# The first two k-tiles' weights on ScalarE's DMA queue, in a one-core encoder block

## Chip, cores and metric

The kernel runs on one core of one Trainium2 chip. The metric is device time in microseconds (us): the median of 3 runs of the whole program, 980.93 us for the kernel before (980.78 to 981.23).

## The reference

One layer of a streaming encoder on 512 positions with 1024 channels (`x` is 1 x 512 x 1024, float32). Cut to its start, which is where the change lies:

```
hn   = rms_norm(h, g_mix_pre)             # h = x, per position over 1024 channels
proj = hn @ w_in                          # 1024 x 8192, split among the mixers
a, gate = split(z_conv); h_conv = a * sigmoid(gate)     # columns 2048..4095 of w_in
...   # spatial gating, causal conv of width 31, multi-scale pooling, three gates,
      # output projection, SwiGLU (2816 wide), per-layer input embedding
```

The normalisation's factor is one number per position, so a product with `x * g_mix_pre` can start before it is known and be scaled afterwards. The kernel does that for the first 6 column blocks of the conv projection.

## The kernel before, in words

**Layout.** Channels lie on the 128 partitions, positions (512) on the free axis. A contraction over 1024 channels is 8 k-tiles of 128. TensorE multiplies float32 values as two rounded parts, high and low: each product is three matmuls (high by high, weight-high by x-low, weight-low by x-high), so each weight and each activation tile is split once: ScalarE rounds the high part (`CAST` or `ACTIVATE`), VectorE subtracts to get the low one.

**The start.** TensorE first runs 9 warm-up matmuls on zeros (`ps_warm`, 8 of 512 columns and one of 256). Meanwhile the inputs arrive: `vec` (the gains, L132, issued by ScalarE), 8 k-tiles of x (`x_all`, 256 KB each, L140) and 8 k-tiles of the first weights (`first_all` and `first_raw`, 384 KB each, L143), issued by SyncE in one hand-written order: the table `X_AHEAD = (1, 2, 4, 8, ...)` says how many tiles of x go ahead of each weight tile. The weights of k-tile 0 come in two cuts (128 KB and 256 KB), so that the first two column blocks can start on the smaller. Below, w0a and w0b are these two cuts, w1 the weights of k-tile 1, x0 to x7 the tiles of x; all land in their own place, and a DMA signals one of 8 semaphores (DMAHW0 to DMAHW7) taken in turn in program order, so that the ninth DMA waits until the first has landed.

**The first product.** `first_product(k, passes)` adds k-tile k to six PSUM banks (`ps_first`): six matmuls weight-high by x-high, six weight-high by x-low, six weight-low by x-high, 18 in all. For k-tile 0 the two column blocks of w0a go through all three passes first (6 matmuls), then the four of w0b (12). `x_high(k)` on ScalarE writes the high part of x times gain (`xg`), `x_low(k)` on VectorE the low one, `w_split(k)` splits the weights, `x_square(k)` adds the square of x to the statistics (`sq`, `x_sums`). All of them run in program order on each engine:

```
x_high(1); w_split(1); x_low(1); x_square(1); x_square(2)
first_product(1, passes)
```

So VectorE's order for k-tile 1 is: low part of w1, then low part of xg1; and ScalarE's is xg1 high, then w1 high. After k-tile 3 the statistics go through `ps_stat`, and the program goes on with the other weights, which SyncE loads one block at a time (L199).

Of the kernel before, what the change touches and what calls it, by code (L numbers as in the profile page):

```python
# [85 lines left out]
def hybrid_block(  # L86
# [7 lines left out]
    nc = tc.nc  # L94
# [19 lines left out]
    def slot(tag, name, dt=F32R, shape=(2, T)):  # L114
        return act.tile([P, *shape], dt, tag=tag, name=name, bufs=6 if tag == "tm" else 8)
# [11 lines left out]
    first_raw = []  # L127

    def first_cuts(k):
        return ((0, 2 * P), (2 * P, N_FIRST)) if k == 0 else ((0, N_FIRST),)  # L130
# [3 lines left out]
    for k in range(KT):  # L134
        if k < 5:
            first_raw.append(first_all[:, k * N_FIRST:(k + 1) * N_FIRST])
        else:
            first_raw.append(slot("hn", "first_raw", F32, (D,))[:, :N_FIRST])
        while x_ahead < X_AHEAD[k]:
            nc.sync.dma_start(out=x_all[:, x_ahead], in_=xT[:, x_ahead])  # L140
            x_ahead += 1
        for c0, c1 in first_cuts(k):
            nc.sync.dma_start(out=first_raw[k][:, c0:c1], in_=w_first[k][:, c0:c1])  # L143

    def col(name, k):
        i = VECS.index(name) * KT + k
# [775 lines left out]
    with order():  # L922
# [19 lines left out]
        c0, c1 = ffn_out_cuts[1]  # L942
# [10 lines left out]
        k = 0  # L953
# [92 lines left out]
```

## Time and profile before

| what | value |
|---|---|
| runs | 980.78, 980.93, 981.23 us; median 980.93 |
| profiled execution, own time | 980.2 us |
| its span | 978.4 us |
| TensorE busy | 971.8 us, 99% of the span |
| VectorE, ScalarE busy | 69%, 36% |
| TensorE granted clock | 1.0 in every slice |
| DMA moved | 102.76 MB, mean 105 GB/s |

The span runs from the first to the last instruction that the profiler saw; the run's own time holds 1.8 us more around it. PE is TensorE's matmul, PEld its weight load, DVE VectorE, ACT ScalarE, SP SyncE. All matmuls and splits go through one helper, so they all show line L73, and groups are told apart by tile names (`xg`, `first`, `ps_first`). Times in a timeline are us from the span's start. The ends of matmuls are modelled; the starts of weight loads are the better clock of TensorE's progress.

### The profile page before, as it was taken

The page shows a single profiled execution, that of the slowest core. Times are in us where ns is not written, and L with a number is a line of the kernel's source. Part 1 is how long each engine was busy: PE and PEld are TensorE (multiplying, and loading weights), DVE is VectorE, ACT ScalarE, POOL GpSimd, SP SyncE. Part 2 cuts the span into 40 slices and gives each one's busy share as a digit, 9 for nine tenths or more (in the row PEclk, how much of TensorE's full clock was granted, in tenths as well). Part 3 has the DMA queues.
Part 4 walks back from the last instruction along what each step waited for, and adds up shares of the span by engine and source line. Part 5 has one row for each costly group of instructions (what it writes and reads, how often), then busy time and mean ns, then how long its engine had stood idle before and what let it go on. Part 6 is the DMA issues. An engine that isn't in the chain of part 4 may idle for free.

```text
span 978.4 us, 11730 instructions
## 1 busy us (share of the span) xinstructions
PE 971.8 (99%) x4683; PEld 818.0 (84%) x4683; DVE 672.4 (69%) x905; ACT 350.4 (36%) x487; POOL 83.8 (9%) x63
## 2 busy tenths in 40 slices
PE   9999999999999999999999999999999999999998
PEld 6888888788888888888888998888888888888897
DVE  7987789999988899967555777544454432223575
ACT  7522323432214432247326433323232322223442
POOL 1100013000013702160000010000000000000000
PEclk9999999999999999999999999999999999999999
DMA  8723322222222222332337112232323233334312
GB/s 305 195 93 102 113 87 72 100 86 96 99 86 90 96 95 92 102 110 85 108 123 264 45 44 86 88 107 86 108 86 108 84 99 97 100 86 138 110 42 86
DMA packets 30726, 102.76 MB, mean 105 GB/s; under 512 B 3536, under 2 KB 4048, under 8 KB 30672
## 3 DMA queue, kind: packets, MB, share of 16 engines
q1 hardware_dynamic: 29808, 99.75, 31.1%
q0 software_dynamic: 720, 2.23, 1.2%
q8 instruction: 36, 0.59, 0.2%
q14 instruction: 18, 0.15, 0.0%
q10 hardware_dynamic: 144, 0.04, 0.0%
HBM read 97.68 MB, written 2.10 MB: 102 GB/s over the span
## 4 chain that ended last, share of the span: by engine, by line
PE 94%; DVE 4%; issue 1%; ACT 0%
PE ps_f L73 25%; PE ps_gate L73 13%; PE ps_br L73 13%; PE ps_fo L73 12%; PE ps_ag L73 6%; PE ps_pg L73 5%; PE ps_o L73 5%; PE ps_z L73 4%; PE ps_nat L73 4%; PE ps_first L73 3%; DVE lo L73 1%; DVE acc L73 1%; PE ps_ple L73 1%; PE ps_pool L73 1%; DVE v_all L73 1%
## 5 line engine op out<-in xcount | busy, mean ns | idle before, releaser
L73 ACT CAST hi<-raw 128x1024 fp32r<-128x1024 f32 (+2 forms) x157 | 161.6, 1031 | 455.9 <-PE ps_br L73 83.6
L73 DVE TENSOR_TENSOR lo<-raw,hi 128x1024 fp32r<-128x1024 f32 (+2 forms) x155 | 203.9, 1317 | 107.8 <-ACT hi L73 107.3
L73 DVE SCALAR_TENSOR_TENSOR acc<-h_conv,vec,acc 128x511 f32<-128x511 f32 (+14 forms) x240 | 183.4, 764 | 5.2
L73 PE MATMUL ps_f<-hg,hi 128*128 128x512 f32 (+1 forms) x624 | 184.3, 378 | 0.0
L73 PEld LDWEIGHTS ps_f<-hg,hi 128*128 128x128 f32 x624 | 115.1, 188 | 21.8
L73 PE MATMUL ps_gate<-hn,hi 128*128 128x512 f32 x384 | 119.6, 392 | 0.9 <-DVE gated L73 0.9
L73 PE MATMUL ps_f<-hg,lo 128*128 128x512 f32 (+1 forms) x312 | 117.8, 378 | 0.0
L73 PE MATMUL ps_fo<-f,hi 128*128 128x512 f32 (+1 forms) x396 | 111.0, 366 | 0.0
L73 PEld LDWEIGHTS ps_gate<-hn,hi 128*128 128x128 f32 x384 | 71.9, 188 | 17.0 <-DVE gated L73 1.3
L73 PEld LDWEIGHTS ps_fo<-f,hi 128*128 128x128 f32 x396 | 71.7, 189 | 12.2
L73 PE MATMUL ps_nat<-hi,hn 128*128 128x512 f32 x256 | 78.9, 389 | 0.0
L73 PE MATMUL ps_gate<-hn,lo 128*128 128x512 f32 x192 | 74.8, 389 | 0.0
L73 PE MATMUL ps_fo<-f,lo 128*128 128x512 f32 (+1 forms) x198 | 72.4, 365 | 0.0
L73 PEld LDWEIGHTS ps_f<-hg,lo 128*128 128x128 f32 x312 | 58.7, 188 | 10.9
L73 PEld LDWEIGHTS ps_nat<-hi,hn 128*128 128x128 f32 x256 | 48.0, 188 | 10.1
L73 DVE TENSOR_TENSOR f<-ps_f,h_inv 128x512 f32<-128x512 f32 x22 | 15.2, 690 | 56.5 <-PE ps_f L73 56.5
L73 PE MATMUL ps_nat<-lo,hn 128*128 128x512 f32 x128 | 49.8, 389 | 0.0
L73 PE MATMUL ps_ag<-hn,hi 128*128 128x512 f32 x160 | 49.2, 389 | 0.0
L73 PEld LDWEIGHTS ps_gate<-hn,lo 128*128 128x128 f32 x192 | 36.0, 188 | 7.5
L73 PEld LDWEIGHTS ps_fo<-f,lo 128*128 128x128 f32 x198 | 37.3, 189 | 5.9
L73 DVE TENSOR_TENSOR silu<-ps_f,h_inv 128x512 f32<-128x512 f32 x22 | 15.2, 690 | 36.3 <-PE ps_f L73 36.2
L73 PE MATMUL ps_br<-pool,hi 128*128 128x512 f32 x128 | 39.6, 389 | 0.0
(221 smaller groups left out, 1561.2 us busy)
## 6 DMA issues: line engine op xcount, KB each, us to landing
raw<-in_w_mix SPq DMA_DIRECT2D x90, 512.0 KB, 3.3
raw<-in_w_ffn_in SPq DMA_DIRECT2D x44, 512.0 KB, 3.3
raw<-in_w_ffn_out SPq DMA_DIRECT2D x16, 448.0 KB, 3.3
raw<-in_w_ffn_out SPq DMA_DIRECT2D x8, 512.0 KB, 3.6
raw<-in_w_ple_gate SPq DMA_DIRECT2D x8, 512.0 KB, 3.8
x_all<-in_xT SPq DMA_DIRECT2D x8, 256.0 KB, 6.4
h_all<-in_xT SPq DMA_DIRECT2D x4, 512.0 KB, 5.5
out_dram<-pg SPq DMA_DIRECT2D x7, 256.0 KB, 2.0
```

The source lines that it names most:

```text
L73: inst = op(*args, **kw)
```

## The change

For k-tiles 0 and 1 the weight DMAs are issued by ScalarE instead of SyncE. That is three DMAs: w0a, w0b and w1.

```diff
         while x_ahead < X_AHEAD[k]:
             nc.sync.dma_start(out=x_all[:, x_ahead], in_=xT[:, x_ahead])
             x_ahead += 1
+        queue = nc.scalar if k < 2 else nc.sync
         for c0, c1 in first_cuts(k):
-            nc.sync.dma_start(out=first_raw[k][:, c0:c1], in_=w_first[k][:, c0:c1])
+            queue.dma_start(out=first_raw[k][:, c0:c1], in_=w_first[k][:, c0:c1])
```

ScalarE at the program's start, before the change (the number in front is the place in the engine's order; `waits` names semaphores; `xg_126` is xg0, `xg_127` xg1):

```order
1 L132 DMA vec<-in_vecs 128x72
2 L73 ACT_TABLE_LOAD
3 L73 COPY warm<-mean_mat 128x1 [waits DVE_49]
4 L73 ACTIVATE xg_126<-x_all,vec 128x512 [waits DMAHW1_49,DMAHW0_49]
5 L73 CAST first<-first_all 128x512 [waits DMAHW3_49]
6 L73 ACTIVATE x_sums<-x_all 128x512
7 L73 ACTIVATE xg_127<-x_all,vec 128x512 [waits DMAHW4_49]
8 L73 CAST first<-first_all 128x768 [waits DMAHW5_49]
```

ScalarE at the same place with the change:

```order
1 L132 DMA vec<-in_vecs 128x72
2 L144 DMA first_all<-in_w_first 128x256
3 L144 DMA first_all<-in_w_first 128x512
4 L144 DMA first_all<-in_w_first 128x768
5 L73 ACT_TABLE_LOAD
6 L73 COPY warm<-mean_mat 128x1 [waits DVE_49]
7 L73 ACTIVATE xg_126<-x_all,vec 128x512 [waits DMAHW1_49,DMAHW0_49]
8 L73 CAST first<-first_all 128x512 [waits DMAHW5_49]
9 L73 ACTIVATE x_sums<-x_all 128x512
10 L73 ACTIVATE xg_127<-x_all,vec 128x512 [waits DMAHW2_49]
11 L73 CAST first<-first_all 128x768 [waits DMAHW7_49]
```

The three issues stand behind `vec` and ahead of the table load, the warm copy and the first `xg`.

SyncE at the program's start, before the change:

```order
1 L140 DMA x_all<-in_xT 128x512
2 L143 DMA first_all<-in_w_first 128x256
3 L143 DMA first_all<-in_w_first 128x512
4 L140 DMA x_all<-in_xT 128x512
5 L143 DMA first_all<-in_w_first 128x768
6 L140 DMA x_all<-in_xT 128x512 x2
7 L143 DMA first_all<-in_w_first 128x768 [waits DMAHW0_49]
8 L140 DMA x_all<-in_xT 128x512 [waits DMAHW1_49]
9 L140 DMA x_all<-in_xT 128x512 [waits DMAHW2_49]
10 L140 DMA x_all<-in_xT 128x512 [waits DMAHW3_49]
11 L140 DMA x_all<-in_xT 128x512 [waits DMAHW4_49]
12 L143 DMA first_all<-in_w_first 128x768 [waits DMAHW5_49]
```

SyncE at the same place with the change:

```order
1 L140 DMA x_all<-in_xT 128x512 x4
2 L144 DMA first_all<-in_w_first 128x768 [waits DMAHW0_49]
3 L140 DMA x_all<-in_xT 128x512 [waits DMAHW1_49]
4 L140 DMA x_all<-in_xT 128x512 [waits DMAHW2_49]
5 L140 DMA x_all<-in_xT 128x512 [waits DMAHW3_49]
6 L140 DMA x_all<-in_xT 128x512 [waits DMAHW4_49]
7 L144 DMA first_all<-in_w_first 128x768 [waits DMAHW5_49]
```

x0 to x3 now stand next to each other; behind them the order of SyncE's DMAs is as before. The semaphores of the first eight DMAs are dealt out in another order (x1 takes DMAHW2, x2 DMAHW4, x3 DMAHW6, w0a DMAHW3, w0b DMAHW5, w1 DMAHW7); the rows from the ninth on wait for the same numbers as before. The orders of TensorE, VectorE and GpSimd are unchanged.

## Rows read from the trace of the kernel before

**Rows 1.** The page: busy time by engine, the granted clock in 40 slices, and the chain that ended last, by engine.

```profile
PE 971.8 (99%) x4683; PEld 818.0 (84%) x4683; DVE 672.4 (69%) x905; ACT 350.4 (36%) x487; POOL 83.8 (9%) x63
...
PEclk9999999999999999999999999999999999999999
...
PE 94%; DVE 4%; issue 1%; ACT 0%
```

**Rows 2.** The chain in order of time, 0 to 45 us: start us, us, what.

```profile
1.34 3.81 PE ps_warm L73 x9
5.14 15.38 PE ps_first L73 x66
20.52 0.86 PE ps_stat L73 x2
```

**Rows 3.** Timeline of PEld: start us, us, operation, and in brackets the idle time before it with what ended it. The first rows are of 1 to 6 us; the others are the 19th and the 25th weight load of the first product, each asked for by its own short stretch.

```profile
1.74 0.15 PEld L73 LDWEIGHTS <-warm_up 128*128 128x128 bf16 x1 [0.28 <-issue]
2.16 0.15 PEld L73 LDWEIGHTS <-warm_up 128*128 128x128 bf16 x1 [0.28 <-issue]
...
4.81 0.50 PEld L73 LDWEIGHTS ps_first<-xg,first 128*128 128x128 f32 x2 [0.36 <-ACT xg L73]
5.71 14.38 PEld L73 LDWEIGHTS ps_first<-xg,first 128*128 128x128 f32 x64 [0.40 <-DVE xg L73]
...
9.25 0.19 PEld L73 LDWEIGHTS ps_first<-xg,first 128*128 128x128 f32 x1
...
10.61 0.19 PEld L73 LDWEIGHTS ps_first<-xg,first 128*128 128x128 f32 x1
```

**Rows 4.** Timeline of ScalarE, 0 to 9 us, same columns (ACTq is its DMA issue).

```profile
0.74 0.41 ACTq L132 DMA_DIRECT2D vec<-in_vecs  x1
1.18 1.28 ACT L73 ACT_TABLE_LOAD   x1 [1.18 <-PEq L1034]
2.47 0.19 ACT L73 COPY warm<-mean_mat 128x1 f32<-128x1 f32 x1
4.04 0.72 ACT L73 ACTIVATE xg<-x_all,vec 128x512 fp32r<-128x512 f32 x1 [1.38 <-DMA vec<-in_vecs]
4.88 0.62 ACT L73 CAST first<-first_all 128x512 fp32r<-128x512 f32 x1
...
7.00 0.72 ACT L73 ACTIVATE xg<-x_all,vec 128x512 fp32r<-128x512 f32 x1 [0.96 <-DMA x_all<-in_xT]
7.98 0.83 ACT L73 CAST first<-first_all 128x768 fp32r<-128x768 f32 x1 [0.26 <-DMA first_all<-in_w_first]
```

**Rows 5.** Timeline of VectorE, 3 to 11 us, same columns.

```profile
4.24 0.29 DVE L73 CAST first<-first_all 128x256 fp32r<-128x256 f32 x1 [2.56 <-DMA first_all<-in_w_first]
4.57 0.43 DVE L73 TENSOR_TENSOR first<-first_all,first 128x256 fp32r<-128x256 f32 x1
4.92 0.75 DVE L73 SCALAR_TENSOR_TENSOR xg<-x_all,vec,xg 128x512 fp32r<-128x512 f32 x1
...
8.85 0.96 DVE L73 TENSOR_TENSOR first<-first_all,first 128x768 fp32r<-128x768 f32 x1 [2.58 <-ACT first L73]
9.72 0.74 DVE L73 SCALAR_TENSOR_TENSOR xg<-x_all,vec,xg 128x512 fp32r<-128x512 f32 x1
```

**Rows 6.** Timeline of SyncE's DMA issues, 0 to 12 us, its first ones: start us, us, what, how many.

```profile
0.74 0.39 SPq L140 DMA_DIRECT2D x_all<-in_xT  x1
1.19 0.90 SPq L143 DMA_DIRECT2D first_all<-in_w_first  x2
2.12 0.43 SPq L140 DMA_DIRECT2D x_all<-in_xT  x1
2.60 0.43 SPq L143 DMA_DIRECT2D first_all<-in_w_first  x1
3.07 0.91 SPq L140 DMA_DIRECT2D x_all<-in_xT  x2
4.03 0.42 SPq L143 DMA_DIRECT2D first_all<-in_w_first  x1
```

**Rows 7.** DMA issues by line in short stretches: queue, how many, KB each, us from issue to landing. In order: x0 (issued at 0.74), w0a (1.19), vec (0.74); w0b (1.66); x1 and w1 (2.12 and 2.60, in one answer); w2 and x3 (4.03 and 3.55, in one answer).

```profile
x_all<-in_xT SPq DMA_DIRECT2D x1, 256.0 KB, 3.1
first_all<-in_w_first SPq DMA_DIRECT2D x1, 128.0 KB, 3.0
vec<-in_vecs ACTq DMA_DIRECT2D x1, 36.0 KB, 3.3
...
first_all<-in_w_first SPq DMA_DIRECT2D x1, 256.0 KB, 3.2
...
first_all<-in_w_first SPq DMA_DIRECT2D x1, 384.0 KB, 5.4
x_all<-in_xT SPq DMA_DIRECT2D x1, 256.0 KB, 4.9
...
first_all<-in_w_first SPq DMA_DIRECT2D x1, 384.0 KB, 6.7
x_all<-in_xT SPq DMA_DIRECT2D x1, 256.0 KB, 6.2
```

**Rows 8.** DMA traffic. First, what was moved in each of 40 slices of 0 to 10 us (0.25 us each, GB/s); then the two queues in the stretch 2.5 to 3.0 us (q1 is SyncE's, q10 ScalarE's): packets, MB, share of the 16 DMA engines.

```profile
GB/s 0 0 0 0 0 0 0 158 100 226 232 330 367 314 371 393 328 197 49 131 197 160 217 270 332 377 356 324 295 295 307 262 287 332 328 352 414 418 406 414
...
q1 hardware_dynamic: 80, 0.12, 71.5%
q10 hardware_dynamic: 63, 0.02, 15.1%
```

**Rows 9.** Timeline of PE, 184 to 190 us: an idle stretch before a matmul and the matmuls after it.

```profile
185.52 0.72 PE L73 MATMUL ps_gate<-hn,hi 128*128 128x512 f32 x2 [0.88 <-DVE gated L73]
186.08 0.40 PE L73 MATMUL ps_gate<-hn,lo 128*128 128x512 f32 x1
186.31 0.62 PE L73 MATMUL ps_gate<-hn,hi 128*128 128x512 f32 x2
```

**Rows 10.** The page's groups of ScalarE, the table loads of the whole program: how many, busy us, mean ns of one.

```profile
L73 ACT ACT_TABLE_LOAD x8 | 10.3, 1283 | 15.7 <-DVE silu L73 13.3 <-PE ps_pg L73 1.2 <-PEq L1034 1.2
```

**Rows 11.** Timeline of VectorE, 15.5 to 19 us: the low part of w3, and that of xg3.

```profile
15.67 0.96 DVE L73 TENSOR_TENSOR first<-first_all,first 128x768 fp32r<-128x768 f32 x1
...
17.94 0.75 DVE L73 SCALAR_TENSOR_TENSOR xg<-x_all,vec,xg 128x512 fp32r<-128x512 f32 x1
```

## The prediction, made before the changed kernel was run

> **What bounds the kernel now.** I read the page first: TensorE is busy 99% of the span, the chain that ended last is 94% TensorE, and the granted clock is full in every slice [rows 1]. So a start that comes earlier or later moves the end by as much, unless TensorE gives it back in a later wait, and there is hardly one. The chain in order of time shows the start: warm-up matmuls from 1.34 to 5.14 us, then 66 matmuls of the first product in one piece, the statistics, and on [rows 2]. The timeline of the weight loads tells how tight that piece is: the engine waits 0.36 us for xg0 (high part) at 4.81 and 0.40 us for its low part at 5.71, and from there 64 weight loads follow each other in 14.38 us, 0.225 us each, without a wait [rows 3]. From 5.71 on TensorE is never short of data. That is the frame: the change can gain at most what those two waits cost, and it can lose wherever a DMA that now lands later eats the slack of a later step.
>
> **The most that can be gained.** The first wait is worth nothing: the load at 4.81 stands beside a warm-up matmul that runs until 5.14 [rows 2, 3]. It ended with xg0, which waited on `vec` (landing at 0.74 + 3.3 = 4.04) and not on any DMA that moves [rows 4, 7]. The second ended with xg0's low part, 4.92 + 0.75 = 5.67 on VectorE, behind the low part of w0a, 4.57 to 5.00, behind w0a's landing at 1.19 + 3.0 = 4.19 [rows 5, 7]. With w0a earlier, that step would still wait for xg0's high part, 4.04 + 0.72 = 4.76 [rows 4]: 0.16 us before the 4.92 at which it now starts. So the gain is at most 0.16 us, and it holds only if nothing behind it becomes late.
>
> **What ScalarE pays.** Three issues go ahead of its table load. SyncE's issues stand 0.45 to 0.48 us apart (0.74, 1.19, then two in 0.90, 2.12, 2.60) [rows 6], and ScalarE's own took 0.41 with the next instruction 0.03 later [rows 4]. So the table load starts at about 1.18 + 3 x 0.46 = 2.56 instead of 1.18, lasts 1.28 (the mean over eight of them is 1283 ns, most of them in the thick of weight traffic) [rows 10], and the copy (0.19) ends at 4.04. ScalarE was idle 1.38 us before xg0 [rows 4]; the move of 1.38 uses up all of it and no more. I cost it at nothing; its bounds are 0 and 0.1 us. If each issue were slower than 0.46, the excess, three times, would go straight into xg0.
>
> **When the DMAs are issued.** w0a and w0b keep their issue times (1.18 and 1.65 against 1.19 and 1.66), w1 comes at 2.1 instead of 2.60, and x1 to x3 come at 1.19, 1.66 and 2.12 instead of 2.12, 3.07 and 3.55 [rows 6]. x1's high part has slack already: ScalarE has it at 7.72, and it is used at 9.25 [rows 3, 4]. Behind x3, SyncE's order is the old one; w2 waits for `vec` until 4.04 and goes out where it did, 4.03. I cost this at nothing, and it is not this that decides.
>
> **What decides: who shares the DMA engines.** Before, one queue held x0, w0a, w0b, x1, w1, x2, x3 in the order in which TensorE wants them. Now two queues run side by side, with x0, x1, x2, x3 in one and vec, w0a, w0b, w1 in the other. In the one stretch in which both queues had work, 2.5 to 3.0 us, SyncE's moved 80 packets and ScalarE's 63 [rows 8]: they took turns, nearly packet for packet. Each of these tiles is 128 rows on 16 engines, the same number of packets for x as for weights. So w1, fourth in its queue, comes through when the fourth of the other queue does, x3, where before it stood two tiles of x ahead of it. The old trace gives both ends: w1 landed at 2.60 + 5.4 = 8.0 (ScalarE started on it at 7.98 [rows 4]), x3 at 3.55 + 6.2 = 9.75 [rows 7]. Bytes moved up to that point are the same, so 9.75 is the late bound. The early bound is 7.98: the traffic has a hole at 4.25 to 5.75 us, with 49 to 217 GB/s between stretches of over 330 [rows 8], although SyncE alone had issued seven DMAs by 4.0 [rows 6]. Two queues may fill it. Six slices that average 159 instead of 340 are 181 GB/s x 1.5 us = 270 KB, or 0.8 us at 340 GB/s; so filled wholly, x3 and w1 land at about 8.95, and w1 may still come out a little ahead of x3. I take 8.8.
>
> The Trainium skill speaks against the change here: "DMA: Bandwidth & Descriptors", section "Issuing engines are not separate DMA queues", says that DMAs started by different engines interleave on the same 16 DMA engines, and that starting them from several saves only the issuing time. The packet counts of rows 8 agree. Taken alone, the rule leaves nothing that could fill the hole, and the time would be that of the late bound below.
>
> **What a late w1 costs.** From its landing, ScalarE takes 0.83 for the high part, VectorE starts the low part at +0.87 and that of xg1 at +1.74, done at +2.48 (7.98, 8.85, 9.72, 10.46) [rows 4, 5]. TensorE wants the high part at the 19th weight load, 9.25, and xg1's low part at the 25th, 10.61 [rows 3]. The slack is 9.25 - 8.81 = 0.44 us and 10.61 - 10.46 = 0.15 us. The second binds: TensorE comes late by (landing of w1) - 8.13. At 8.8 that is **0.7 us**; at 9.75 it is 1.6; at 7.98 nothing. Behind it, everything that hangs on w1 moves along with TensorE. k-tile 3 has little slack (xg3's low part is done at 18.69, and its place by the 0.227 us steps from the 25th load on is 36 x 0.227 = 8.17 later, 18.78), but it follows w3's landing [rows 11], which comes behind the same bytes as before, and a TensorE that is 0.7 later gives it more room.
>
> w0b has two rivals in the other queue as well, so it may land up to 0.6 us later than 1.66 + 3.2 = 4.86 [rows 7]; its high part is done 0.62 after ScalarE takes it, about 6.1, and TensorE wants it after six matmuls, at 5.71 + 4 x 0.225 = 6.6 [rows 3]. Covered. w0a may land later too, by up to 0.6; each tenth delays the start by a tenth, but this does not add to w1's delay, which is counted from fixed landing times.
>
> **Sum.** Gain 0 (at most -0.16), ScalarE's issue 0, w1 +0.7 (0 to 1.6): +0.7 us. The profiled execution took 980.2, so it would be 980.9; the median of the runs stands 0.73 higher, so the forecast is 980.93 + 0.7 = **981.6 us**. About 0.2%, 1.96 us, is what a measurement of this kernel can tell from no change; the forecast lies inside.
>
> **Rivals.**
> - *The two queues fill the hole.* w1 lands no later than 8.13, TensorE stays fed, and the low part of xg0 starts up to 0.16 sooner: 980.8 to 980.9. For it: the hole is real [rows 8]. Against: w1 has to overtake two of the three tiles of x that share with it.
> - *The start stalls and the clock stays low* (slower). The warm-up's weight loads stand 0.42 us apart for 512 columns, the later ones 0.225 [rows 3]: TensorE ran at its 1.2 GHz level then and at 2.4 afterwards, with the warm-up busy up to the change, while the granted clock reads full in both. If w0a lands 0.5 us late, or ScalarE's issues take 0.2 us longer each, TensorE is idle from 5.14 on, and the rise may come only after another stretch of work. At the low level the first product's remaining 16 matmuls take 16 x (0.42 - 0.225) = 3.1 us more: 984.0 us. Against: after an idle 0.88 us at 185.5 us the matmuls kept their short steps [rows 9], though after long work.
> - *The change does not do what it says.* The three DMAs do stand in ScalarE's order, ahead of the table load, so this has no weight.
> - *Faster by over 0.2%*: no wait of 2 us is there to be removed.
>
> **How the numbers follow.** Late w1 (+0.2 to +1.6): 0.58. The hole filled, no loss: 0.30. Low clock: 0.10. Something else that gains over 0.2%: 0.02. The first two lie within 0.2%. The range takes both, from 980.93 - 0.16 to 980.93 + 1.6, and 0.3 on each side for the spread of the runs (980.78 to 981.23): 980.5 to 982.8.
>
> **What would show it.** In the changed profile: three issues on ScalarE from 1.18 to about 2.55, xg0 still at 4.0 to 4.1, w1's high part starting at 8.3 to 9.75 instead of 7.98, and weight loads of `ps_first` with waits on `first` and on xg1's low part near 9.3 and 10.6, of 0.7 us together. Wrong if the loads run through without a wait (the hole was filled), if xg0 starts after 4.3 (issues are dearer than I take them), or if the loads after 5.7 stand 0.4 us apart (the clock).

## The result, and the profile after

The changed kernel takes 982.6 us (981.48 to 983.31, 22 runs) against 980.8 us (980.23 to 981.65, 22 runs): +1.8 us, ratio 1.0017, interval 1.0012 to 1.0023. That is inside the range and on the forecast's side of the kernel before, but 2.5 times the 0.7 us that were forecast, and the profile shows that it was not lost where the forecast put it. The profiled execution took 982.99 us, its span 981.2 us, 2.8 us over that of [rows 1 to 11]. The two profiles stand a little apart from their medians (980.2 against 980.8 us before, 982.99 against 982.6 after), which is why they differ by 2.8 us and the medians by 1.8.

ScalarE in the changed kernel, 0 to 10 us (start us, us, operation, idle time before it and what ended that; ACTq is its DMA issue), to be held against [rows 4]:

```profile
0.74 0.42 ACTq L132 DMA_DIRECT2D vec<-in_vecs  x1
1.19 1.42 ACTq L144 DMA_DIRECT2D first_all<-in_w_first  x3
2.63 1.28 ACT L73 ACT_TABLE_LOAD   x1 [2.63 <-issue]
3.93 0.19 ACT L73 COPY warm<-mean_mat 128x1 f32<-128x1 f32 x1
4.29 0.72 ACT L73 ACTIVATE xg<-x_all,vec 128x512 fp32r<-128x512 f32 x1 [0.17 <-DMA vec<-in_vecs]
7.43 0.62 ACT L73 CAST first<-first_all 128x512 fp32r<-128x512 f32 x1 [2.43 <-DMA first_all<-in_w_first]
...
9.11 0.81 ACT L73 CAST first<-first_all 128x768 fp32r<-128x768 f32 x1
```

The issues cost what was counted: table load at 2.63, copy done at 4.12, and then 0.17 us of waiting for `vec`, so ScalarE itself delayed nothing. w0b (the 128x512 row) is split at 7.43 instead of 4.88, w1 at 9.11 instead of 7.98.

VectorE in the changed kernel, the same columns, against [rows 5]:

```profile
5.63 0.29 DVE L73 CAST first<-first_all 128x256 fp32r<-128x256 f32 x1 [3.95 <-DMA first_all<-in_w_first]
6.30 0.75 DVE L73 SCALAR_TENSOR_TENSOR xg<-x_all,vec,xg 128x512 fp32r<-128x512 f32 x1
...
10.83 0.74 DVE L73 SCALAR_TENSOR_TENSOR xg<-x_all,vec,xg 128x512 fp32r<-128x512 f32 x1
```

w0a is the one that hurts: VectorE starts on it at 5.63 instead of 4.24, 1.4 us later. The weight loads of TensorE, against [rows 3]:

```profile
4.30 0.15 PEld L73 LDWEIGHTS <-warm_up 128*128 128x128 bf16 x1 [0.28 <-issue]
6.04 0.50 PEld L73 LDWEIGHTS ps_first<-xg,first 128*128 128x128 f32 x2 [1.59 <-issue]
7.10 15.78 PEld L73 LDWEIGHTS ps_first<-xg,first 128*128 128x128 f32 x64 [0.56 <-DVE xg L73]
```

Two losses stand here. The third load comes at 7.10 instead of 5.71: 1.39 us. And the 64 loads from there take 15.78 us instead of 14.38: 1.40 us, with no wait among them. Together 2.79, the 2.8 us of the span. Read one by one, the loads from 7.27 to 9.83 stand 0.43 us apart, the pace of the warm-up (512 columns in 0.43 us is the 1.2 GHz level), and from 10.2 on 0.23. The column of the granted clock reads 1.00 all through; the pace of the loads is what tells.

DMA traffic, 0 to 10 us in slices of 0.25 us, and the two queues at 4 to 5 us (q1 is SyncE's, q10 ScalarE's), against [rows 8]; then the issues with their time to landing, against [rows 7]: first ScalarE's (w1, w0b, w0a, `vec`), then x1, x2 and x3 (issued at 1.18, 1.65 and 2.12):

```profile
GB/s 0 0 0 0 0 0 0 156 166 194 167 277 252 247 333 383 377 344 299 307 389 352 369 324 299 348 315 373 385 447 369 406 434 397 406 397 406 406 410 393
...
q1 hardware_dynamic: 109, 0.19, 56.4%
q10 hardware_dynamic: 124, 0.14, 38.2%
...
first_all<-in_w_first ACTq DMA_DIRECT2D x1, 384.0 KB, 6.9
first_all<-in_w_first ACTq DMA_DIRECT2D x1, 256.0 KB, 5.7
first_all<-in_w_first ACTq DMA_DIRECT2D x1, 128.0 KB, 4.4
vec<-in_vecs ACTq DMA_DIRECT2D x1, 36.0 KB, 3.5
...
x_all<-in_xT SPq DMA_DIRECT2D x1, 256.0 KB, 4.2
...
x_all<-in_xT SPq DMA_DIRECT2D x1, 256.0 KB, 5.6
...
x_all<-in_xT SPq DMA_DIRECT2D x1, 256.0 KB, 6.7
```

The hole at 4.25 to 5.75 us is gone, as one rival supposed. It did not help, for the bytes that came sooner were not those that TensorE waited for: w0a took 4.4 us from issue to landing instead of 3.0. The two queues took turns (109 and 124 packets in 1 us), and each weight tile landed about 0.2 us behind the tile of x that has the same place in the other queue: w0a at 5.6 behind x1 at 5.4, w0b at 7.4 behind x2 at 7.2, w1 at 9.0 behind x3 at 8.8. The traffic was also thinner at first: 247 to 277 GB/s at 2.75 to 3.5 us, where [rows 8] have 314 to 367.

### The profile page after: what moved, and what is told of

Read it like the earlier page. It is cut to its first block, busy times and chain, and to the rows that moved or that the text cites. A ratio compares the mean times of both kernels' runs of the same rounds, so it can differ in the third digit from the quotient of the medians.

```text
span 981.2 us, 11730 instructions
## 1 busy us (share of the span) xinstructions
PE 973.7 (99%) x4683; PEld 819.3 (83%) x4683; DVE 672.3 (69%) x905; ACT 350.2 (36%) x487; POOL 83.9 (9%) x63
## 4 chain that ended last, share of the span: by engine, by line
PE 94%; DVE 4%; issue 1%; DMA 0%; ACT 0%; ACTq 0%
PE ps_f L73 25%; PE ps_gate L73 13%; PE ps_br L73 13%; PE ps_fo L73 12%; PE ps_ag L73 6%; PE ps_pg L73 5%; PE ps_o L73 5%; PE ps_z L73 4%; PE ps_nat L73 4%; PE ps_first L73 4%; DVE lo L73 1%; DVE acc L73 1%; PE ps_ple L73 1%; PE ps_pool L73 1%; DVE v_all L73 1%
```

## The experiments

The theory after the result, T1: taking turns with the other queue makes w0a late, TensorE falls idle behind the warm-up, and its clock stays low for some us after that idle time. The rival T2 is the forecast's own: the late w1. All ratios are to the kernel before.

**w1 alone on ScalarE's queue.**

```diff
-        queue = nc.scalar if k < 2 else nc.sync
+        queue = nc.scalar if k == 1 else nc.sync
```

> Only w1 is issued by ScalarE, right behind vec; w0a and w0b stay in SyncE's queue behind x0. Theory T1 (the loss comes from w0a, which lands 1.4 us later behind vec in a queue that takes turns with x, and from TensorE's clock, which stays low after the idle time that this opens): w0a lands near 4.2 us again, the first weight load of the first product stands near 4.8, and the time is that of the kernel before within 0.4 us. Theory T2 (my forecast: w1 in the shared queue is what comes late): w1 is now second in its queue and should land by about 7, so T2 too expects no loss; a loss of over 0.7 us would speak for a third cause, ScalarE's issue or the sharing as such.

Measured: 981.18 us, ratio 1.0010 (1.0001 to 1.0019). Eight of the 11 runs lie at 980.87 to 981.35, three at 982.76 to 983.0 (none of those three was profiled). By the medians it is 0.6 us above the kernel before, where T1 had expected at most 0.4 and T2 no loss. T1 as written was wrong on one point: w0a was late here too. VectorE, PEld, and the DMA traffic from 0 to 10 us in slices of 0.25 us:

```profile
5.40 0.29 DVE L73 CAST first<-first_all 128x256 fp32r<-128x256 f32 x1 [3.72 <-DMA first_all<-in_w_first]
...
5.81 0.30 PEld L73 LDWEIGHTS ps_first<-xg,first 128*128 128x128 f32 x2 [1.36 <-ACT xg L73]
6.87 14.38 PEld L73 LDWEIGHTS ps_first<-xg,first 128*128 128x128 f32 x64 [0.76 <-DVE xg L73]
...
GB/s 0 0 0 0 0 0 0 164 172 209 207 100 128 153 246 419 419 377 414 365 430 402 410 393 402 410 385 385 393 434 459 414 393 361 389 385 377 393 402 401
```

w0a was back in SyncE's queue, behind x0 alone, and still landed 1.16 us later than before. w1, now second on the other queue, was through right behind it (1.17 + 4.6 = 5.8 us), so much of w1 had gone ahead of w0a's last bytes. And the traffic was thin: 100 to 153 GB/s at 2.75 to 3.5 us, so that 430 KB, the size of x0, `vec` and w0a, had moved by 3.95 us instead of 3.5 [rows 8]; that is 0.45 of the 1.16 us. So it isn't ScalarE's queue that is slow; a second queue with work delays the first as well. And here, after the idle time, the 64 loads took 14.38 us, the fast pace.

**w0a and w0b alone on ScalarE's queue.**

```diff
-        queue = nc.scalar if k < 2 else nc.sync
+        queue = nc.scalar if k == 0 else nc.sync
```

> Only w0a and w0b are issued by ScalarE; w1 stays in SyncE's queue behind x0 and x1. T1: w0a lands near 5.6 us as in the changed kernel, TensorE idles about 0.9 us behind the warm-up, its first loads stand 0.43 us apart, and the time is the changed kernel's, +1.4 to +2.2 us over the kernel before. T2: w1 is early, so no loss, within 0.4 us of the kernel before.

Measured: 982.69 us, ratio 1.0019 (1.0011 to 1.0028), the changed kernel's time, as T1 has it and T2 does not: w1 landed at 8.3 us here, 0.3 later than before. PEld:

```profile
5.58 0.50 PEld L73 LDWEIGHTS ps_first<-xg,first 128*128 128x128 f32 x2 [1.13 <-ACT xg L73]
6.64 1.35 PEld L73 LDWEIGHTS ps_first<-xg,first 128*128 128x128 f32 x4 [0.56 <-DVE xg L73]
9.14 14.18 PEld L73 LDWEIGHTS ps_first<-xg,first 128*128 128x128 f32 x60 [1.15 <-ACT first L73]
```

The start is late by 0.93 us (6.64 against 5.71), four loads take 1.35 us (slow pace), and the third wait, 1.15 us, is for w0b, which landed 6.8 us after its issue against 3.2 before. w0b is late too, and T1 had not named it.

**w0a ahead of vec on ScalarE's queue.**

```diff
-    nc.scalar.dma_start(out=vec[:, :N_VEC], in_=vecs[:, :N_VEC])
...
+            if k < 2:
+                with order():
+                    act_e.dma_start(out=first_raw[k][:, c0:c1], in_=w_first[k][:, c0:c1])
+                    if k == 0 and c0 == 0:
+                        act_e.dma_start(out=vec[:, :N_VEC], in_=vecs[:, :N_VEC])
...
```

> The changed kernel with w0a as the first DMA in ScalarE's queue and vec as the second, order forced. If w0a was late because it stood behind vec's 128 short rows in a queue that takes turns with x0: w0a lands at 3.6 to 4.2 us, vec at 4.3 to 4.8, xg0 starts by then, the first weight load stands at 5.1 to 5.6, and one half to all of the loss goes, 0 to +0.9 us over the kernel before. If the sharing with x as such made it late: w0a still lands after 5 us and the time stays within 0.4 us of the changed kernel's. With the start mended, w1, landing near 9.0 us, would be the next to bind by T2's arithmetic: a start delay of 9.05 - 8.13 = 0.9 us.

Measured: 982.85 us, ratio 1.0020 (1.0011 to 1.0029): nothing was mended. ScalarE, VectorE, PEld:

```profile
5.43 0.72 ACT L73 ACTIVATE xg<-x_all,vec 128x512 fp32r<-128x512 f32 x1 [1.31 <-DMA vec<-in_vecs]
...
4.42 0.29 DVE L73 CAST first<-first_all 128x256 fp32r<-128x256 f32 x1 [2.74 <-DMA first_all<-in_w_first]
...
6.99 15.52 PEld L73 LDWEIGHTS ps_first<-xg,first 128*128 128x128 f32 x64 [0.29 <-DVE xg L73]
```

w0a was in time for once (4.42), but `vec`, second in the queue, landed 1.3 us later than before and took its place as the late one. The first expectation was right on w0a, the second on the time. Whichever tile stood second in this queue was late.

**SyncE's other tiles held back.** The weights stay on ScalarE's queue; x1 gets a dependence on a one-column copy behind w0a's landing, and SyncE's DMAs are kept in program order.

```diff
+    sp = order.engine(nc.sync)
+    with order():
+        dve.tensor_copy(x_all[:, 1, :1], warm)
...
+                sp.dma_start(out=x_all[:, x_ahead], in_=xT[:, x_ahead])
...
```

> The changed kernel, but SyncE issues x1 and everything behind it only once w0a has landed: x1 waits for a one-column copy into its place, which VectorE runs behind the first split of w0a. The three weight DMAs stay on ScalarE's queue. If taking turns with x1 to x3 is what made w0a late: w0a lands near 4.2 us as in the kernel before, w0b by 5.5, the first loads stand at 4.8 and 5.7 and 0.23 us apart, and the time is within 0.5 us of the kernel before (some of that is at risk, since x1 to x7 and w2 now come about 2 us later). If ScalarE's queue is slower by itself: w0a still lands after 5 us and the time stays at +0.9 to +2 us.

Measured: 990.2 us (4 runs), ratio 1.0098, where 0.5 us at most had been expected. The total says nothing on the question: x1 now lands at 9.2, and keeping SyncE's order made later weight loads late (waits at `ps_o` and `ps_pg`, far from the start). The start does answer it:

```profile
4.29 0.29 DVE L73 CAST first<-first_all 128x256 fp32r<-128x256 f32 x1 [2.61 <-DMA first_all<-in_w_first]
...
4.86 0.30 PEld L73 LDWEIGHTS ps_first<-xg,first 128*128 128x128 f32 x2 [0.47 <-ACT xg L73]
5.76 0.76 PEld L73 LDWEIGHTS ps_first<-xg,first 128*128 128x128 f32 x4 [0.60 <-DVE xg L73]
```

With nothing of SyncE's but x0 beside it, w0a landed 3.1 us after its issue on ScalarE's queue and the third load stood at 5.76, as before the change. w0b was not back in place (split at 6.15 instead of 4.88). The control with one queue further down has it at 6.34, so this much lateness of w0b does not need a second queue; its cause was not followed up.

**A late w1 by itself**, on the kernel before with its one queue.

```diff
-X_AHEAD = (1, 2, 4, 8, 8, 8, 8, 8)
+X_AHEAD = (1, 4, 4, 8, 8, 8, 8, 8)
```

> The kernel before, one queue, with x2 and x3 issued ahead of w1. w0a, w0b and the start stay as they were; w1 lands where x3 did, near 9.7 us. This measures the price of a late w1 by itself, the term on which my forecast rested. T2's arithmetic (lateness = landing - 8.13): TensorE stalls before the 19th and the 25th weight load, 1.6 us together, and the time is +1.6 us. If the stall of about 1.2 us before the 19th load also costs clock, up to 1.5 us more. If there was more slack than I counted: under +0.5 us.

Measured: 982.3 us, ratio 1.0018 (1.0008 to 1.0027), +1.6 us. ScalarE and PEld:

```profile
9.97 0.83 ACT L73 CAST first<-first_all 128x768 fp32r<-128x768 f32 x1 [1.64 <-DMA first_all<-in_w_first]
...
10.86 1.23 PEld L73 LDWEIGHTS ps_first<-xg,first 128*128 128x128 f32 x6 [1.33 <-ACT first L73]
12.51 9.39 PEld L73 LDWEIGHTS ps_first<-xg,first 128*128 128x128 f32 x42 [0.43 <-DVE xg L73]
```

9.97 - 8.13 = 1.84 us by the forecast's arithmetic; the two waits are 1.33 and 0.43, 1.76 together, and the span grew by 1.8 (980.2). The price was right. Behind this wait, at 10.86 us, the loads kept the fast pace.

**The warm-up cut short**, no DMA moved.

```diff
-N_WARM = 8
+N_WARM = 5
```

> The kernel before with 5 long warm-up matmuls instead of 8; no DMA moves. The warm-up then ends near 3.7 us, and TensorE idles about 1.1 us before its first weight load at 4.81, as it idles 0.9 us in the changed kernel. If the idle time is what keeps the clock low: loads 0.43 us apart for some 3 us after the start, and +1 to +2.5 us over the kernel before. If the clock does not mind such a gap: loads 0.23 us apart from the third on, and a time within 0.3 us of the kernel before.

Measured: 981.63 us, ratio 1.0011 (1.0002 to 1.0020). PEld:

```profile
4.86 0.50 PEld L73 LDWEIGHTS ps_first<-xg,first 128*128 128x128 f32 x2 [1.69 <-ACT xg L73]
5.73 15.77 PEld L73 LDWEIGHTS ps_first<-xg,first 128*128 128x128 f32 x64 [0.37 <-DVE xg L73]
```

The start is where it was (5.73), the DMAs too, and yet the 64 loads take 15.77 us, 1.39 more than before and just what the changed kernel's took. The medians differ by 0.95 us, a little under the 1 to 2.5 that were expected. A shorter warm-up with an idle us behind it is enough; this run does not tell the missing work from the idle time. In the changed kernel the warm-up was whole, and only the idle time was added.

**The changed kernel with a longer warm-up.**

```diff
-N_WARM = 8
+N_WARM = 12
```

> The changed kernel with 12 long warm-up matmuls instead of 8, so that TensorE has work until about 6.0 us, when w0a's high part is ready. T1 with the clock: the first loads stand 0.23 us apart at once, the start is 1.2 to 1.4 us late and no more, and the time is 0.5 to 1.4 us below the changed kernel's, though TensorE does more work. Rival (the slow loads are not due to the idle time but to the data or to the DMA traffic beside them): loads still 0.43 us apart, and the time is the changed kernel's or up to 0.3 us above it.

Measured: 981.72 us, ratio 1.0010 (1.0002 to 1.0019), all 11 runs between 981.12 and 982.03. PEld:

```profile
6.00 0.15 PEld L73 LDWEIGHTS <-warm_up 128*128 128x128 bf16 x1 [0.28 <-issue]
6.43 1.34 PEld L73 LDWEIGHTS ps_first<-xg,first 128*128 128x128 f32 x6 [0.28 <-issue]
8.24 13.49 PEld L73 LDWEIGHTS ps_first<-xg,first 128*128 128x128 f32 x60 [0.47 <-ACT first L73]
```

The slow stretch is gone and 0.6 us of the loss with it (1.2 us over the kernel before by the medians, instead of 1.8), though TensorE does more. None of the 11 runs lies above 982.03 us, and 15 of the 22 of the changed kernel do. What stays is the late start and a wait of 0.47 us for w0b.

**The longer warm-up on the kernel before**, the same edit, as a control.

> The kernel before with 12 long warm-up matmuls instead of 8, no DMA moved: a control for the run with the longer warm-up. The warm-up ends near 6.0 us and pushes the first product, whose inputs are ready at 4.8 and 5.7, to about 6.0. If TensorE's start alone sets the end: +0.8 to +1.2 us over the kernel before, about what the changed kernel with the same warm-up showed. If the longer warm-up gave something back in clock: below +0.5 us.

Measured: 980.9 us, ratio 1.0003 (0.9994 to 1.0012): no loss, where I expected about 1 us. PEld, then ScalarE:

```profile
4.30 0.97 PEld L73 LDWEIGHTS <-warm_up 128*128 128x128 bf16 x5 [0.28 <-issue]
5.39 1.23 PEld L73 LDWEIGHTS ps_first<-xg,first 128*128 128x128 f32 x6
7.01 13.49 PEld L73 LDWEIGHTS ps_first<-xg,first 128*128 128x128 f32 x60 [0.39 <-ACT first L73]
...
6.34 0.62 ACT L73 CAST first<-first_all 128x512 fp32r<-128x512 f32 x1 [1.59 <-DMA first_all<-in_w_first]
```

Five warm-up loads from 4.30 on fit into 0.97 us: here the clock rose at 4.3 us, and the first product began at 5.4, not 6.0. In the run above, the same warm-up still ran at the slow pace at 6.00. The moment of the rise differs between these two executions by some 2 us. The wait of 0.39 us is for w0b: split at 6.34 instead of 4.88, although every tile but `vec` is on one queue here. So w0b's landing differs by 1.5 us between two executions with the same DMAs on one queue, and not all of its lateness in the runs above is the change's. In the traces with w1 or w0b on ScalarE's queue and x1 not held back it was split at 6.4 to 8.5, always later than with one queue (4.9 to 6.3).

**The changed kernel three more times, one profile each.** Its 22 runs seem to lie in two groups (8 up to 982.2 us, 14 from 982.5 on), which this was to explain.

> The changed kernel once more, for one profile. Its 22 runs lie in two groups, 8 at 981.5 to 982.2 us and 14 at 982.5 to 983.3. Theory: the groups differ by whether TensorE's clock had risen before the warm-up ended. If so, a run below 982.2 shows loads 0.23 us apart from its first products on, and a run above 982.4 shows some three us of loads 0.43 us apart, with w0a landing at 5.0 to 5.7 us in both. Rival: the groups differ by when w0a or w0b lands, and the pace of the loads is the same in both.

> As the look before: time above 982.4 us with slow loads, or below 982.2 with fast ones; the rival expects equal pace and another landing of w0a or w0b.

> As the two looks before: time above 982.4 us with slow loads, or below 982.2 with fast ones; the rival expects equal pace and another landing of w0a or w0b.

Measured: 982.91, 982.08 and 982.99 us. All weight loads between 5 and 10 us, count, busy us, mean ns, idle before; of the first execution, then of the second:

```profile
L73 PEld LDWEIGHTS ps_first<-xg,first 128*128 128x128 f32 x11 | 3.3, 323 | 2.5 <-ACT xg L73 1.3 <-DVE xg L73 0.6
```

```profile
L73 PEld LDWEIGHTS ps_first<-xg,first 128*128 128x128 f32 x14 | 2.4, 188 | 3.3 <-ACT xg L73 1.5 <-DVE xg L73 0.8 <-ACT first L73 0.7
```

The warm-up and the wait for w0b in the second execution:

```profile
1.33 3.52 PE L73 MATMUL ps_warm<-warm_up 128*128 128x512 bf16 x9 [1.33 <-DVE warm_up L73]
...
8.48 13.48 PEld L73 LDWEIGHTS ps_first<-xg,first 128*128 128x128 f32 x60 [0.66 <-ACT first L73]
```

The third execution is like the first (10 loads, mean 318 ns). The second, 0.8 us faster, is the one with fast loads, although w0a landed later in it (split at 5.58 against 5.29 in the first) and TensorE waited longer. Its warm-up took 3.52 us instead of 3.81 [rows 2], so its clock had risen before the idle time. In these three it is the pace of the loads that goes with the time, and not the landing; that all 22 runs divide by it was not shown.

## Why the prediction was right in its direction and wrong in its place

- **The frame held.** TensorE's start sets the end: the start's 2.79 us are the span's 2.8.
- **The gain was nothing, as said**, and ScalarE's issues cost nothing: the pitch was 0.48 instead of 0.46, and xg0 still waited for `vec`, which landed 0.2 us later. xg0 started at 4.29, and at 4.34 to 4.68 in the three repeats; the forecast's sign "after 4.3" for dear issues would mislead there, since it was `vec` that was late.
- **Turns between the queues: right.** The packet counts and the pairs of landings of the changed kernel show it, and holding back the other queue's tiles undoes it for w0a.
- **The step that failed** is the sentence that w0a "may land later too, by up to 0.6" and that this "does not add". No row stood behind the 0.6. The count by which w1 comes through with x3 was not applied to w0a: behind `vec`, it comes through with x1. x0, `vec`, x1 and w0a are some 690 KB, and the slices of the changed kernel reach that at 4.4 us; the 430 KB of x0, `vec` and w0a had moved by 3.5 before [rows 8]. By this count w0a would be 0.9 us late, an estimate; in the four traces of the changed kernel it was split 1.05 to 1.39 us late, and the rest is not accounted for. About 0.2 of the 0.9 us is the thinner traffic (430 KB by 3.7 us). The same holds for w0b: 0.6 us was allowed for, 2.5 measured, of which one queue alone can show 1.5, as the control does. It binds in the second repeat (0.66 us) and with w0 alone (1.15 us).
- **The term of 0.7 us for w1 measured nothing here.** w1's price was right, as the run with w1 alone late shows, and its landing nearly (forecast 8.8, landed at 9.0, split at 9.11). But the start had become 1.4 us later, and with it the 19th and 25th loads, so w1 was covered: xg1's low part was done at 10.83 + 0.74 = 11.57 us, and the 25th load stood at 13.41. Two of the forecast's own signs of being wrong appeared: the 64 loads ran through without a wait, and after 5.7 us they stood 0.4 us apart. That the total still came out on the side of the forecast and near it is luck: the one term it was made of cost nothing, and a late w0a, put at nothing, with the slow clock, a rival at 0.10, cost 2.8 us in the profile. The forecast's late bound, 980.93 + 1.6 = 982.5 us, lies near the measured 982.6 by chance too: w1 landed at 9.0, not at 9.75.
- **The slower rival took place, in three of the four traces.** It had 0.10. Its mechanism (idle from 5.14 on, clock still low, slow loads) is what the profile shows; its price was 3.1 us, and the slow stretch cost 1.40, since the clock rose some 3 us after the third load, when 7 loads had been slow, and not all 16. The evidence that I held against it, the fast matmuls behind an idle 0.88 us [rows 9], was of another kind: there the clock was high before the gap, as in the run with the late w1. Cutting the warm-up short shows the slow loads without any DMA moved; lengthening it takes them away.
- **The sum by what was measured**: the second repeat, with a late start, a wait for w0b and no slow loads, has a span of 980.3, +1.9; with slow loads 981.1 to 981.2, +2.7 to +2.8. In the median of the runs the change costs 1.8 us, and in the run with the longer warm-up, which has the late start and the wait for w0b but no slow loads, 1.2.

In these traces an execution has the slow stretch when the clock had not risen before the idle time, and the moment of the rise moves between executions: 4.3 us in one, after 6.0 in another, with the same warm-up from 1.34 us on. The Trainium skill, "TensorE: Matmul & The Clock Gate", section "Part 1: The HAM clock gate (the "warmup" mystery)", says that the moment of the change isn't tied to the kernel's start. The traces agree in that. Why w0b landed late when SyncE's tiles were held back, and with one queue in the control, is open. A version faster than the kernel before did not show itself: the most there was to gain at the start is 0.16 us, which these runs can't tell from nothing.

## What to carry to other kernels

In these traces one queue delivered in the order of its issues, so that order was a priority; a second queue took about every other packet, so what stood second on either came later, however early it was issued. Before moving a DMA to another queue, count for each tile that the critical engine waits for, the very first ones above all, how many tiles of the other queue come through ahead of it. And a warm-up must last until the first data can be late: a gap between it and the work costs its own length and can cost a stretch of slow clock as well, 1.4 us here.

## What was not expected of the hardware

With one queue, 49 to 217 GB/s were moved at 4.25 to 5.75 us while SyncE alone had issued seven DMAs [rows 8]; in the changed kernel no slice from 3.5 us on is below 299. The other traces divide the same way: in the three further runs with all of these tiles on one queue the lowest slice between 4 and 6 us has 82, 98 and 107 GB/s, and in those with w1 or w0b on ScalarE's queue and x1 not held back none there is below 299. Why one queue leaves that hole was not tried. Earlier it is the other way round: at 2.75 to 3.5 us the mean was 127 to 305 GB/s in those traces and 337 to 361 with one queue, and x0, the first tile of its own queue, came a little later too in the changed kernel (3.3 us from issue to landing instead of 3.1). Why was not tried either. The granted clock's column read 1.00 in stretches in which the loads stood 0.43 us apart.
